# Attention in units twice as large, with masks as products, in a streaming-encoder step

## The chip, the cores and the metric

The kernel runs on one core of a Trainium2 chip. The metric is the device time of one execution in microseconds (us), from the first instruction to the last, with what the launch puts around it. PE is TensorE (matrix products), DVE is VectorE, ACT is ScalarE, POOL is GpSimd and SP is SyncE, which here only issues DMAs. PSUM, where PE writes, has eight banks of 128 partitions by 512 fp32 numbers.

## The reference, cut to what matters

One inference step over 256 prompt frames and 8 streams of 16 frames (384 rows in three blocks of 128; the third holds the streams) goes through a Mamba-2 layer and a PEER layer (a mixture of 16384 single-row experts), then an attention layer and a second PEER layer. Only attention changes:

```python
kv = rmsnorm(h, norm_kv) @ a_w_kv + a_b_kv        # 4 KV heads of 64
q = xn @ a_w_q[j] + a_b_q[j]                      # 16 query heads, 4 for each KV head
# prompt: chunks of 64 frames, a chunk sees itself and the two before it
scores = einsum('bcqkgd,bcskd->bckgqs', qb, kb) * scale
probs = sink_softmax(where(valid, scores, -inf), sinks)   # one more logit per head: the sink
out = einsum('bckgqs,bcskd->bcqkgd', probs, vb)
# streams: 16 queries against 128 cached rows and the 16 new ones
mix = o @ a_w_o[j] + a_b_o[j]
```

## The kernel before, in words

`mamba`, `peer(0)`, `attention`, `peer(1)` and `final` follow each other. A large fp32 product is made of three fp32r products, with each operand split into a high and a low part (`split`, L105 on ACT and L106 on DVE); their products are 128x128 weights against 256 to 512 moving columns and are called wide here. A framework orders the instructions of each engine in advance from its own estimate of their durations; those in `pin(...)` keep the order in which they are written, among themselves.

A PEER layer ends with 128 steps over the second expert table (`v_step`, products on L143) mixed with gathered rows for the streams (`v_quad`, L1089) and, in its first half, with sums that DVE makes of gathered rows (L1072) and of one-hot rows (`w_step`, L1111 to L1133). Near its end `h`, which was spilled to HBM, is read back (L1228).

Attention normalises `h`, transposes it and makes keys and values (`kv_block`, L143), then query tiles of 128 columns (`q_tile`, L130 to L132, 24 wide products each). POOL issues the loads of its constants first of all (L609 to L622): biases, sinks, the cached keys `ck` and values `cv`, and the output bias row `bo`. The body of attention goes over units. A prompt unit is two of the four query heads of a KV head, for one block of 128 rows, with 128 or 256 keys; there are 16. A unit of a stream is two KV heads with their eight query heads, 128 rows against 256 keys; there are 16. Each unit has `scores` (L719 on 64 of the 128 rows of the array; L728 and L729 on 64 rows and 64 columns), the mask addition on DVE out of PSUM into `sm` (L722, L731), `softmax` (maximum L693 on DVE, exponentials L700 on ACT, division L705 on DVE), `transposes` four units later (L741, copied out by ACT on L744) and `values` five units later (L758 and L771, weights of 64 columns). These products are called narrow here, and the transposes are counted with them. Six query tiles are written between the first scores. At the end the output projection runs (wide, L143 with `ohi`).

Of the kernel before, what the change touches and what calls it, by code (L numbers as in the profile page):

```python
# [9 lines left out]
F32 = mybir.dt.float32  # L10
# [9 lines left out]
P = 128  # L20
# [38 lines left out]
def encoder_step(ctx: ExitStack, tc: tile.TileContext, t_in, t_out):  # L59
# [543 lines left out]
    def attention():  # L603
        with ExitStack() as c:
# [4 lines left out]
            pool.dma_start(bq, t_in["b_q"])  # L609
            bkv = brow(t_in["b_kv"], 512, one, "bkv", pool)  # L610
            snk = brow(t_in["sinks"], 16, one, "snk", pool)
            nsnk = T(one, [P, 16], F32, tag="nsnk")
            dve.tensor_scalar(nsnk, snk, -1.0, None, op0=OP.mult)
            snks = T(one, [P, 2], F32, tag="snks")
            pool.dma_start(snks, t_in["sinks_s"])
            nsnks = T(one, [P, 2], F32, tag="nsnks")
            dve.tensor_scalar(nsnks, snks, -1.0, None, op0=OP.mult)
            ck = T(one, [64, NSEQ, 4, P], F32, tag="ck")
            cv = T(one, [P, NSEQ, 256], F32, tag="cv")
            pool.dma_start(ck, t_in["ckT"])  # L620
            pool.dma_start(cv, t_in["cache_v"].rearrange("s k d -> k s d"))
            bo = brow(t_in["b_o"], D, one, "bo", pool)  # L622

            mask0 = T(one, [P, P], F32, tag="mask0")
            pool.memset(mask0, 0.0)
            pool.memset(mask0[0:64, 64:128], NEG)
            mask1 = T(one, [P, NP], F32, tag="mask1")
            pool.memset(mask1, 0.0)
            pool.memset(mask1[0:64, 192:256], NEG)
            pool.memset(mask1[64:128, 0:64], NEG)  # L630
            maskS = T(one, [P, NSEQ, NP], F32, tag="maskS")
# [14 lines left out]
            r = rstd_of(h, DONE)  # L646
            accs = [[bank([P, 512])] for _ in range(NB)]
# [42 lines left out]
            def softmax(sm, sink, nsink, nh, nk):  # L690

                nm = T(two, [P, 2], F32, tag="nm", bufs=6)[:, :nh]
                dve.tensor_reduce(nm, sm, axis=AX.X, op=OP.max)  # L693
                dve.scalar_tensor_tensor(nm, nm, -0.125, nsink, op0=OP.mult, op1=OP.min)
                es = T(two, [P, 2], F32, tag="es", bufs=6)[:, :nh]
                dve.tensor_tensor(es, sink, nm, op=OP.add)
                act.activation(es, es, AF.Exp)
                den = T(two, [P, 2], F32, tag="den", bufs=6)[:, :nh]
                for i in range(nh):
                    act.activation(sm[:, i], sm[:, i], AF.Exp, bias=nm[:, i:i + 1], scale=0.125,  # L700
                                   accum_out=den[:, i:i + 1])
                dve.tensor_tensor(den, den, es, op=OP.add)
                dve.reciprocal(den, den)
                for i in range(nh):
                    dve.tensor_scalar(sm[:, i], sm[:, i], den[:, i:i + 1], None, op0=OP.mult)  # L705


            P_, PT = {}, {}
            LAG = 4

            def scores(u):
                kind, i, n, par = u
                sm = T(two, [P, 512], F32, tag="sm", bufs=LAG + 2)
                if kind == "p":
                    nk = (P, NP)[i]
                    hf = slice(64 * par, 64 * par + 64)
                    ps = bank([P, 2, nk])
                    for j in range(2):
                        pe.matmul(ps[:, j], qT[hf, 2 * n + j, i * P:(i + 1) * P], kT[hf, n, 0:nk],  # L719
                                  start=True, stop=True)  # L720
                    sm = sm[:, :2 * nk].rearrange("p (n k) -> p n k", k=nk)
                    dve.tensor_tensor(sm, ps, (mask0, mask1)[i].unsqueeze(1).to_broadcast([P, 2, nk]), op=OP.add)  # L722
                    softmax(sm, snk[:, 4 * n + par:4 * n + 4:2], nsnk[:, 4 * n + par:4 * n + 4:2], 2, nk)
                else:
                    ps = bank([P, NP])
                    for h2 in range(2):
# [620 lines left out]
```

## Time and profile before

| | |
|---|---|
| three runs | 2575.7, 2599.0, 2598.19 us; median 2598.19 us |
| the profiled execution | 2597.6 us, its span 2595.9 us |
| TensorE's granted clock, mean | 0.976 of 2.4 GHz |
| PE busy | 2449.1 us, 94% |
| DVE busy | 1941.7 us, 75% |
| ACT busy | 1323.8 us, 51% |
| POOL busy | 685.0 us, 26% |
| body of attention, first scores to output projection | 1440.57 to 1547.80 us |

In the table of stretches a row gives the stretch, its length, the busy time of each engine with the number of instructions in brackets, TensorE's granted clock as a share of 2.4 GHz, the share of time in which the DMA engines were busy, and what they moved. The clock has two levels, so 0.79 is a mean over time at 1.00 and at 0.50. In the rows by time, the second number is the duration with its drain; the time to the start of the next row is what a group costs PE when nothing waits.

### The profile page before, as it was taken

How to read it: one execution, taken by the hardware profiler on the slowest of the kernel's cores; microseconds unless marked ns; L12 is line 12 of the kernel's file. 1: busy time of each engine (PE TensorE's matmuls, PEld its weight loads, DVE VectorE, ACT ScalarE, POOL GpSimd, SP SyncE). 2: the span in 40 equal slices, each digit the busy share in tenths (PEclk: the TensorE clock that was granted, in tenths of full speed). 3: DMA queues.
4: the chain of work that ended last, by engine and by line, in shares of the span. 5: the costliest groups of instructions: out<-in, count | busy, mean ns of one | idle time of the engine just before them, and what ended most of it. 6: DMA issues, size and time to landing. Idle time of an engine off the chain costs nothing. (4 is left out here: it accounts for less than half of the span.)

```text
span 2595.9 us, 45141 instructions
## 1 busy us (share of the span) xinstructions
PE 2449.1 (94%) x16792; PEld 2070.4 (80%) x16792; DVE 1941.7 (75%) x4301; ACT 1323.8 (51%) x2562; POOL 685.0 (26%) x749
## 2 busy tenths in 40 slices
PE   7999999999899989999998999999899998899998
PEld 7999988988799966666666878998789976666666
DVE  6877737989899988765545655989989988775545
ACT  5655524433466665554444543434456666464444
POOL 2222200033322244333321100023332234433331
PEclk9999999999999999999998969999999999999999
DMA  4544444488888899888985204478888898988886
GB/s 182 203 148 178 144 135 145 151 282 273 271 305 293 292 340 349 330 308 296 322 307 179 92 9 150 137 253 280 269 286 287 296 323 311 364 294 294 321 315 233
DMA packets 179116, 645.62 MB, mean 249 GB/s; under 512 B 24192, under 2 KB 26096, under 8 KB 176240
## 3 DMA queue, kind: packets, MB, share of 16 engines
q1 hardware_dynamic: 99632, 366.90, 40.2%
q0 software_dynamic: 79264, 275.84, 30.5%
q8 instruction: 131, 2.15, 0.3%
q14 instruction: 89, 0.73, 0.1%
HBM read 626.43 MB, written 18.06 MB: 248 GB/s over the span
## 5 line engine op out<-in xcount | busy, mean ns | idle before, releaser
L105 ACT CAST hi<-raw 128x1024 fp32r<-128x1024 f32 (+1 forms) x616 | 641.3, 1042 | 652.8 <-PE bank L131 407.4
L106 DVE TENSOR_TENSOR lo<-raw,hi 128x1024 fp32r<-128x1024 f32 (+1 forms) x616 | 748.8, 1216 | 225.2 <-ACT hi L105 213.6
L1035 POOL DMA_INDIRECT gath<-in_p_u,eidU x256 | 301.9, 1179 | 803.3 <-DVE gath L1072 438.8
L132 PE MATMUL bank<-xhi,lo 128*128 128x256 f32 (+1 forms) x1344 | 407.5, 304 | 9.9 <-DVE lo L106 9.7
L130 PE MATMUL bank<-xhi,hi 128*128 128x256 f32 (+1 forms) x1344 | 402.3, 299 | 4.2 <-ACT hi L105 4.2
L131 PE MATMUL bank<-xlo,hi 128*128 128x256 f32 (+1 forms) x1344 | 396.7, 295 | 0.0
L132 PE MATMUL bank<-qhi,lo 128*128 128x256 f32 (+1 forms) x1152 | 348.9, 305 | 27.1 <-DVE lo L106 26.9
L130 PE MATMUL bank<-qhi,hi 128*128 128x256 f32 (+1 forms) x1152 | 348.1, 302 | 20.4 <-ACT hi L105 13.6
L1072 DVE SCALAR_TENSOR_TENSOR gath<-gath,xg 128x1024 f32<-128x1024 f32 x256 | 311.5, 1217 | 44.0 <-DMA gath<-in_p_u,eidU 43.9
L131 PE MATMUL bank<-qlo,hi 128*128 128x256 f32 (+1 forms) x1152 | 343.9, 299 | 0.0
L143 PE MATMUL bank<-lo,phi 128*128 128x512 f32 x1024 | 332.3, 406 | 10.2 <-DVE lo L106 8.2
L143 PE MATMUL bank<-hi,plo 128*128 128x512 f32 x1024 | 323.9, 398 | 0.0
L143 PE MATMUL bank<-hi,phi 128*128 128x512 f32 x1024 | 292.8, 406 | 19.4 <-ACT hi L105 16.1
L105 ACT CAST phi<-G 128x256 fp32r<-128x256 f32 x256 | 103.4, 405 | 382.0 <-PE bank L143 264.4
L1035 POOL DMA_INDIRECT gv<-in_p_v,eidT x180 | 202.1, 1123 | 319.0 <-PE bank L1089 273.6
L132 PEld LDWEIGHTS bank<-xhi,lo 128*128 128x128 f32 x1344 | 253.8, 189 | 18.0 <-DVE lo L106 14.1
L143 PEld LDWEIGHTS bank<-hi,phi 128*128 128x128 f32 x1024 | 186.9, 190 | 98.7 <-ACT hi L105 45.6
L130 PEld LDWEIGHTS bank<-xhi,hi 128*128 128x128 f32 x1344 | 254.3, 189 | 8.6 <-ACT hi L105 5.6
L131 PEld LDWEIGHTS bank<-xlo,hi 128*128 128x128 f32 x1344 | 254.1, 189 | 0.2
L132 PEld LDWEIGHTS bank<-qhi,lo 128*128 128x128 f32 x1152 | 222.9, 194 | 34.0 <-DVE lo L106 33.7
L143 PEld LDWEIGHTS bank<-lo,phi 128*128 128x128 f32 x1024 | 187.4, 190 | 73.2 <-DVE lo L106 18.3
L130 PEld LDWEIGHTS bank<-qhi,hi 128*128 128x128 f32 x1152 | 223.7, 194 | 24.3 <-ACT hi L105 16.7
(340 smaller groups left out, 3949.0 us busy)
## 6 DMA issues: line engine op xcount, KB each, us to landing
raw<-in_u_t SPq DMA_DIRECT2D x256, 512.0 KB
raw<-in_p_v SPq DMA_DIRECT2D x256, 512.0 KB
raw<-in_w_in SPq DMA_DIRECT2D x32, 512.0 KB
raw<-in_p_w_q SPq DMA_DIRECT2D x32, 512.0 KB
s<-in_state_ssm SPq DMA_DIRECT2D x8, 1024.0 KB
raw<-in_w_z SPq DMA_DIRECT2D x16, 512.0 KB
out_sm_ssm<-s SPq DMA_DIRECT2D x8, 1024.0 KB
raw<-in_w_out SPq DMA_DIRECT2D x16, 512.0 KB
```

The source lines that it names most:

```text
L105: act.copy(hi, raw)
L106: dve.tensor_tensor(lo, raw, hi32, op=OP.subtract)
L130: pe.matmul(ps, whi[:, s], xhi[:, k, c0:c1], start=(k == 0), stop=False)
L131: pe.matmul(ps, whi[:, s], xlo[:, k, c0:c1], start=False, stop=False)
L132: pe.matmul(ps, wlo[:, s], xhi[:, k, c0:c1], start=False, stop=(k == KD - 1))
L143: mm = pe.matmul(ps, x, w[:, hf * n:(hf + 1) * n], start=s_, stop=e_)
L1035: pool.indirect_dma_start(out=tile_, out_offset=None, in_=tab, in_offset=bass.IndirectOffsetOnAxis(ap=idx, axis=0))
L1072: pin(dve.scalar_tensor_tensor(tile_, tile_, 1.0, xg[g], op0=OP.mult, op1=OP.mult, accum_out=au[g][:, j:j + 1]))
```

## The change

A unit is twice as large: a prompt unit holds all four heads of a KV head, with a PSUM bank for the heads of each row half, and a unit of streams holds two streams in one bank; 16 units are left. Transposes come two units later and values three. The masks are bf16, and PE adds them: an identity (`idb`) times the mask starts the accumulation in the bank, and the scores go on top. DVE takes the maximum and ACT the exponentials straight from PSUM. Prompt scores alternate between the row halves of the array, values between its column halves, and the products of streams likewise. Of the two PSUM copies behind the transposes of a prompt unit DVE makes one. The products of units are pinned in the order masks, transposes, scores, values; query tiles stand behind units 0, 1, 3, 5, 7 and 8. The loads of constants are issued behind the normalisation's POOL work, and the masks are built before. The buffers of the output projection are reserved earlier.

```diff
-            bq = T(one, [P, 8], F32, tag="bq")
-            pool.dma_start(bq, t_in["b_q"])
...
+            def constants():
...
+                pin(pool.dma_start(bq, t_in["b_q"]))
+                row(bkv, t_in["b_kv"])
+                row(snk, t_in["sinks"])
+                pin(pool.dma_start(snks, t_in["sinks_s"]))
+                pin(pool.dma_start(ck, t_in["ckT"]))
+                pin(pool.dma_start(cv, t_in["cache_v"].rearrange("s k d -> k s d")))
+                row(bo, t_in["b_o"])
+            idb = T(one, [P, P], BF16, tag="idb")
+            dve.tensor_copy(idb, ident)
+            mask0 = T(one, [P, 2, P], BF16, tag="mask0")
...
             r = rstd_of(h, DONE)
+            constants()
+            dve.tensor_scalar(nsnk, snk, -1.0, None, op0=OP.mult)
+            dve.tensor_scalar(nsnks, snks, -1.0, None, op0=OP.mult)
...
+            LAG = 2
+            def masks(u):
+                kind, i, n = u
+                if kind == "p":
+                    m = (mask0, mask1)[i]
+                    SC[u] = [bank(m.shape) for _ in range(2)]
+                else:
+                    m = maskS[:, 2 * i:2 * i + 2]
+                    SC[u] = [bank([P, 2, NP])]
+                for ps in SC[u]:
+                    pin(pe.matmul(ps, idb, m, start=True, stop=False))
+            def scores(u):
+                kind, i, n = u
+                pss = SC.pop(u)
+                if kind == "p":
+                    nk = (P, NP)[i]
+                    for j in range(2):
+                        for par in range(2):
+                            hf = slice(64 * par, 64 * par + 64)
+                            pin(pe.matmul(pss[par][:, j], qT[hf, 2 * n + j, i * P:(i + 1) * P], kT[hf, n, 0:nk],
+                                          start=False, stop=(j == 1)))
...
+                for q, ps in enumerate(pss):
+                    dve.tensor_reduce(nm[:, q], ps, axis=AX.X, op=OP.max)
...
+                        act.activation(sm[:, j], ps[:, j], AF.Exp, bias=nm[:, q, j:j + 1], scale=0.125,
+                                       accum_out=den[:, q, j:j + 1])
...
+            def transposes(u):
+                for q, sm in enumerate(P_.pop(u)):
+                    pt = bank([P, 2, nkb, P])
...
+                    if q:
+                        dve.tensor_copy(pT, pt)
+                    else:
+                        act.copy(pT, pt)
...
+                    po = bank([P, 2, P])
                     for j in range(2):
+                        for kb in range(nkb):
+                            for h2 in range(2):
+                                pin(pe.matmul(po[64 * h2:64 * h2 + 64, j], kv[:, kb, 256 + n * 64:256 + (n + 1) * 64],
+                                              pT[h2][:, j, kb], start=(kb == 0), stop=(kb == nkb - 1)))
...
+            q_at = {0: 2, 1: 3, 3: 4, 5: 5, 7: 6, 8: 7}
...
+            for i in range(len(todo) + LAG + 1):
...
+                if i < len(todo):
+                    masks(todo[i])
+                if 0 <= i - LAG < len(todo):
+                    transposes(todo[i - LAG])
+                if i < len(todo):
+                    scores(todo[i])
+                if 0 <= i - LAG - 1 < len(todo):
+                    values(todo[i - LAG - 1])
+                if i in q_at:
+                    q_tile(q_at[i])
```

Three places show how the order moves, names with the numbers of their buffers. On PE, before, the last of the six query tiles (L130 to L132) ends early in the body, and narrow products alone follow it; the scores of nine and a half of the 16 prompt units and of all 16 units of streams are still to come, and the transposes and values of most:

```order
L131 MATMUL bank_15891<-xlo_2733_15298,hi_15894 128x384
L132 MATMUL bank_15891<-xhi_2732_15297,lo_15895 128x384
L719 MATMUL bank_15931<-kT_15261,qT_15257 128x256
L741 MATMUL bank_15948<-ident_69,sm_15712 128x128 x4
L758 MATMUL bank_15955<-pT_15871,kv_15258 64x128
L758 MATMUL bank_15955<-pT_15928,kv_15258 64x128
L758 MATMUL bank_15959<-pT_15871,kv_15258 64x128
L758 MATMUL bank_15959<-pT_15928,kv_15258 64x128
L719 MATMUL bank_15964<-kT_15261,qT_15257 128x256 x2
```

Every row from the third on is narrow, up to the output projection.

Now, on PE behind the last but one query tile (bank_16075, written behind unit 7); L717 is the mask, L770 a transpose, L727 a score:

```order
L132 MATMUL bank_16075<-xhi_2733_15299,lo_16079 128x384
L717 LDWEIGHTS idb_15230
L717 MATMUL bank_16109<-mask_2711_15232,idb_15230 128x256
L717 LDWEIGHTS idb_15230
L717 MATMUL bank_16110<-mask_2711_15232,idb_15230 128x256
L770 MATMUL bank_16113<-ident_69,sm_16007 128x128 x4
L727 MATMUL bank_16109<-kT_15254,qT_15250 128x128
L727 MATMUL bank_16110<-kT_15254,qT_15250 128x128
```

The query tiles now lie among the first nine units; the last one follows this unit, and seven units of scores come behind it. The masks come ahead of the transposes, and the scores go to two banks in turn.

On POOL at the border of the first PEER layer and attention, before:

```order
L1035 DMA gv_14923<-in_p_v,eidT_4013 128x1024
L609 DMA bq_15221<-in_b_q 128x8
L81 DMA bkv_15223<-in_b_kv 128x512
L81 DMA snk_15225<-in_sinks 128x16
L615 DMA snks_15229<-in_sinks_s 128x2
L620 DMA ck_15233<-in_ckT 64x4096
L621 DMA cv_15234<-in_cache_v 128x8x256
L81 DMA bo_15237<-in_b_o 128x1024
L625 MEMSET mask_2710_15239 128x128
```

and now:

```order
L645 MEMSET maskS_15239 128x16 x8
L168 TENSOR_TENSOR rstd_15263<-ss_15261,mhalf_78 128x1 x3
L623 DMA bq_15221<-in_b_q 128x8
L621 DMA bkv_15222<-in_b_kv 128x512
L621 DMA snk_15223<-in_sinks 128x16
L626 DMA snks_15225<-in_sinks_s 128x2
L627 DMA ck_15227<-in_ckT 64x4096
L628 DMA cv_15228<-in_cache_v 128x8x256
L621 DMA bo_15229<-in_b_o 128x1024
L696 DMA out_pr_k<-kv_15251 128x256
```

The loads moved behind all three reciprocal roots (`rstd`), which close the first PEER layer.

The framework also reorders the second PEER layer's last stage, which the edit does not touch. On DVE, in its first half, before:

```order
L106 TENSOR_TENSOR plo_24410<-G_3096_17048,phi_24409 128x256
L1072 SCALAR_TENSOR_TENSOR gath_24293,au_21565<-gath_24293,xg_3113_17093 128x1024
L1111 TENSOR_TENSOR ob_24727<-ioh_76,e1T_17040 128x512
L106 TENSOR_TENSOR lo_24406<-raw_24403,hi_24405 128x1024
L106 TENSOR_TENSOR plo_24453<-G_3096_17048,phi_24452 128x256
```

and now:

```order
L106 TENSOR_TENSOR plo_24204<-G_3001_16842,phi_24203 128x256
L1109 SCALAR_TENSOR_TENSOR gath_24087,au_21359<-gath_24087,xg_3018_16887 128x1024
L1148 TENSOR_TENSOR ob_24521<-ioh_76,e1T_16834 128x512
L106 TENSOR_TENSOR plo_24247<-G_3001_16842,phi_24246 128x256
L1109 SCALAR_TENSOR_TENSOR gath_24164,au_21359<-gath_24164,xg_3018_16887 128x1024
L1170 SCALAR_TENSOR_TENSOR G_3615_20399<-bank_24440,G_3615_20399 128x64x8
L1164 TENSOR_TENSOR oa_24539<-ioh_76,e2T_16835 128x512
L1151 TENSOR_TENSOR og_24523<-ob_24521,g_2998_16836 128x1024
L106 TENSOR_TENSOR lo_24200<-raw_24197,hi_24199 128x1024
```

One low part (`lo`) of an expert row moved behind five other DVE instructions; the rows after it are interleaved in another way too.

## Rows read from the trace of the kernel before

**Rows 1.** Table of stretches: the body of attention and four parts of it.

```profile
1440.57:1547.80 107.23, 104.89 (x769) 80.54 (x768) 68.91 (x266) 58.33 (x210) 0.00 (x0) 0.79 0.11 35
1440.57:1476.50 35.93, 35.93 (x197) 31.49 (x196) 22.90 (x69) 18.43 (x50) 0.00 (x0) 1.00 0.27 88
1476.50:1492.70 16.20, 13.92 (x156) 10.11 (x154) 13.65 (x62) 11.59 (x47) 0.00 (x0) 1.00 0.10 34
1492.70:1537.50 44.80, 44.74 (x244) 30.89 (x244) 27.00 (x111) 21.93 (x88) 0.00 (x0) 0.50 0.00 1
1537.50:1547.80 10.30, 10.30 (x176) 8.04 (x174) 5.35 (x26) 6.39 (x27) 0.00 (x0) 1.00 0.01 3
```

**Rows 2.** Table of stretches: the last 100 products of each PEER layer.

```profile
1369.00:1401.00 32.00, 26.42 (x100) 19.25 (x97) 13.92 (x24) 10.89 (x20) 8.04 (x24) 0.89 0.76 236
2562.60:2587.20 24.60, 23.48 (x100) 17.64 (x96) 14.57 (x23) 11.30 (x20) 1.15 (x2) 1.00 0.56 199
```

**Rows 3.** Waits, 1369 to 1401 us: waiter, what ended it, us, times, longest.

```profile
ACT hi L105 <- DMA raw<-in_p_v: 7.8, 2, 6.2
```

**Rows 4.** Waits, 2562.6 to 2588 us, the second layer's counterpart.

```profile
ACT hi L105 <- DMA raw<-in_p_v: 0.9, 1, 0.9
```

**Rows 5.** PE by time: start, duration, engine, line, names; prompt scores and what follows.

```profile
1445.64 0.71 PE L719 MATMUL bank<-kT,qT 64*128 64x128 f32 x4
1446.28 0.44 PE L130 MATMUL bank<-xhi,hi 128*128 128x384 f32 x1
...
1450.70 1.13 PE L719 MATMUL bank<-kT,qT 64*128 64x256 f32 x4
1451.76 0.45 PE L130 MATMUL bank<-xhi,hi 128*128 128x384 f32 x1
```

**Rows 6.** PE by time: stream scores, transposes and values at the full clock.

```profile
1478.53 0.44 PE L728 MATMUL bank<-ck,qs 64*64 64x128 f32 x4
...
1479.12 0.44 PE L741 MATMUL bank<-ident,sm 128*128 128x128 f32 x2
1479.49 1.09 PE L758 MATMUL bank<-pT,kv 128*64 128x128 f32 x8
1480.51 0.44 PE L728 MATMUL bank<-ck,qs 64*64 64x128 f32 x4
...
1482.40 0.66 PE L758 MATMUL bank<-pT,kv 128*64 128x128 f32 x8
1482.99 0.44 PE L728 MATMUL bank<-ck,qs 64*64 64x128 f32 x4
...
1483.58 0.66 PE L741 MATMUL bank<-ident,sm 128*128 128x128 f32 x4
1484.16 0.44 PE L728 MATMUL bank<-ck,qs 64*64 64x128 f32 x4
```

**Rows 7.** PE by time: wide products of 512 columns, full clock.

```profile
2579.66 0.63 PE L143 MATMUL bank<-lo,phi 128*128 128x512 f32 x2
2580.13 0.63 PE L143 MATMUL bank<-hi,plo 128*128 128x512 f32 x2
```

**Rows 8.** Groups of instructions on DVE, body of attention: busy us, mean ns; idle before.

```profile
L722 DVE TENSOR_TENSOR sm<-bank,mask 128x256 f32<-128x256 f32 (+1 forms) x16 | 8.9, 556 | 11.3 <-PE bank L719 11.3
L731 DVE TENSOR_TENSOR sm<-bank,maskS 128x256 f32<-128x256 f32 x16 | 6.7, 423 | 14.5 <-PE bank L729 14.5
```

**Rows 9.** Groups by form, the same stretch: an exponential and a maximum.

```profile
L700 ACT ACTIVATE sm<-sm,nm 128x256 f32<-128x256 f32 x32 | 16.1, 505 | 4.6 <-DVE nm L694 4.5
L693 DVE TENSOR_REDUCE nm<-sm 128x2 f32<-128x512 f32 x8 | 5.5, 684 | 0.1
```

**Rows 10.** DMA issues, 1360 to 1400 us: one of the constants.

```profile
ck<-in_ckT POOLq DMA_DIRECT2D x1, 1024.0 KB
```

**Rows 11.** Table of stretches: keys and values up to the query tiles.

```profile
1401.00:1430.00 29.00, 24.43 (x107) 19.42 (x105) 20.02 (x35) 16.07 (x30) 1.20 (x3) 0.88 0.32 102
```

**Rows 12.** Table of stretches: the second PEER layer's last stage, first half.

```profile
2104.00:2350.00 246.00, 223.69 (x1470) 151.19 (x1468) 187.92 (x317) 139.90 (x276) 103.58 (x94) 0.99 0.90 327
```

**Rows 13.** Groups by form on DVE, that first half: low parts of expert rows.

```profile
L106 DVE TENSOR_TENSOR lo<-raw,hi 128x1024 fp32r<-128x1024 f32 x59 | 72.2, 1225 | 8.2 <-ACT hi L105 5.7 <-issue 2.4
```

More of the change, by code (lines that the diff above doesn't have):

```diff
@@ L694, in softmax @@
                 dve.scalar_tensor_tensor(nm, nm, -0.125, nsink, op0=OP.mult, op1=OP.min)
-                es = T(two, [P, 2], F32, tag="es", bufs=6)[:, :nh]
                 dve.tensor_tensor(es, sink, nm, op=OP.add)
                 act.activation(es, es, AF.Exp)
[L698 to L701, printed above, removed]
+                sms = []
@@ L703, in softmax @@
                 dve.reciprocal(den, den)
[L704 to L713, printed above, removed]
-                if kind == "p":
[L715 to L726, printed above, removed]
-                        lhs = qs[:, i, 2 * n + h2].rearrange("p g t -> p (g t)")
-                        pe.matmul(ps[64 * h2:64 * h2 + 64, 0:P], lhs, ck[:, i, 2 * n + h2], start=True, stop=True)
-                        pe.matmul(ps[64 * h2:64 * h2 + 64, P:], lhs, kT[0:64, 2 * n + h2, NP:], start=True, stop=True)
-                    sm = sm[:, :NP].rearrange("p (n k) -> p n k", n=1)
-                    dve.tensor_tensor(sm[:, 0], ps, maskS[:, i], op=OP.add)
-                    softmax(sm, snks[:, n:n + 1], nsnks[:, n:n + 1], 1, NP)
-                P_[u] = sm
@@ L735, in transposes @@
-            def transposes(u):
-                sm = P_.pop(u)
-                nh, nkb = sm.shape[1], sm.shape[2] // P
-                pt = bank([P, nh, nkb, P])
-                for j in range(nh):
-                    for kb in range(nkb):
-                        pe.transpose(pt[:, j, kb], sm[:, j, kb * P:(kb + 1) * P], ident)
-                pT = T(two, [P, 512], F32, tag="pT", bufs=4)[:, :nh * nkb * P].rearrange(
-                    "p (n k q) -> p n k q", k=nkb, q=P)
-                act.copy(pT, pt)
-                PT[u] = pT
@@ L753, in values @@
+            def values(u):
+                kind, i, n = u
+                pT = PT.pop(u)
+                if kind == "p":
+                    po = bank([P, 2, P])
                     nkb = (1, 2)[i]
                     for j in range(2):
-                        po = bank([P, P])
-                        for h2 in range(2):
-                            for kb in range(nkb):
-                                pe.matmul(po[64 * h2:64 * h2 + 64, :], kv[:, kb, 256 + n * 64:256 + (n + 1) * 64],
-                                          pT[h2][:, j, kb], start=(kb == 0), stop=(kb == nkb - 1))
@@ L795, in attention, with out_terms @@
-            with tc.tile_pool(name="a3", bufs=1) as late:
-                ohi = T(late, [P, 8, NT], F32R, tag="ohi")
-                olo = T(late, [P, 8, NT], F32R, tag="olo")
+                    todo += [("s", s, n // 2) for s in range(NSEQ // 2)]
+            q_at = {0: 2, 1: 3, 3: 4, 5: 5, 7: 6, 8: 7}
+            late = c.enter_context(tc.tile_pool(name="a3", bufs=1))
+            ohi = T(late, [P, 8, NT], F32R, tag="ohi")
+            olo = T(late, [P, 8, NT], F32R, tag="olo")
+            def out_terms():
@@ L810, in peer @@
+            accs = [[bank([P, 512]) for _ in range(2)] for _ in range(NB)]
+            gemm_row_loop(accs, out_terms())
+            for b in range(NB):
+                for hf in range(2):
+                    hh = h[:, b, hf * 512:(hf + 1) * 512]
+                    dve.tensor_tensor(hh, hh, accs[b][hf], op=OP.add)
     def peer(l):
```

121 lines of the change are left out of this document (61 added, 60 removed).

## The prediction

> **What bounds the kernel now.** The page first: TensorE is busy 94% of the span, so a change elsewhere counts only where PE waits or runs slowly. Then the table of stretches over the part that is edited. The body of attention takes 107.23 us, of which PE is busy 104.89; DVE is busy 68.91 and ACT 58.33 of it, so PE bounds it [rows 1]. The reader should then look at the clock column: 1.00 up to 1492.7 us, 0.50 for 44.8 us, 1.00 after that. PE did 44.74 us of work in the slow part, which is 22.37 us at the full clock. The body is thus 82.5 us of PE work at the full clock (104.89 - 22.37), 2.3 us of idle PE (107.23 - 104.89), and 22.4 us of clock. What PE did before the clock fell is in the same rows: 35.9 us without a gap, query tiles and narrow products mixed, and then 16.2 us of narrow products alone, in which it worked 13.92 us. The second place is the end of the first PEER layer: its last 100 products take 32.0 us, the same 100 in the second layer 24.6 us [rows 2]. The waits say why: ACT waits 7.8 us for rows of the expert table in the first and 0.9 us in the second [rows 3, 4]. The constants of attention load in just that stretch, 1 MB for the cached keys alone [rows 10].
>
> **The sum, against the profiled execution's 2597.6 us** (the median of the runs is 2598.2, so the two agree).
>
> *Constants later.* The seven loads leave the last experts of the first PEER layer. The gain there is the difference of the waits, 6.9 us (7.8 - 0.9); the lengths of the two stretches differ by 7.4. The loads now start behind the third root and run beside keys and values. Their sizes add up to 2.8 MB (1 MB each for keys and values, 0.5 for the output bias, 0.25 for the key-value bias, the rest small); at the 236 GB/s of the border they need 12 us. In the 29 us after it the DMA engines were busy 0.32 of the time [rows 11], which leaves 19.7 us free. So they fit, though some key-value weights will share the engines with them. I charge 1 us and take **-6**; the ends are 0 (all of it given back) and -7.4. The two negations of sinks on DVE now wait for a small load that POOL issues late; behind them stand the low parts of the normalised rows. They are among the first instructions of a stage in which PE has some 5 us of slack (24.43 of 29 busy [rows 11]), and the 1 us covers that.
>
> *Prompt scores.* Two matmuls on one row half cost PE 0.64 us with 128 keys (1446.28 - 1445.64) and 1.06 with 256 [rows 5], and there are two such units for each new one. In the new order the halves alternate. No row shows row halves in turn; the nearest is the value products, where eight records on one column half at a time cost 1.02 us and eight in turn 0.59 [rows 6], a ratio of 0.58. At that ratio a new unit costs 0.74 for 1.28 (saves 0.54) and 1.23 for 2.12 (saves 0.89). Four units of each kind: -5.7. Ends: 0, if row halves don't overlap, and -6.8 at a clean half.
>
> *Values.* Prompt units of 128 keys alternate already in part, so nothing. Those of 256 keys have two such groups of eight, 2 x 1.02, and go to 2 x 0.59: -0.86 each, four units, -3.4. Value products of streams stay as many as before, on halves of 64 columns; nothing. Ends for values: 0 and -4.
>
> *Transposes and scores of streams.* Each group of narrow products ends with a drain. Two transposes cost 0.37 us and four cost 0.58 [rows 6], so joining two groups of two saves 0.16, joining two of four about as much. Twelve units (four with 128 keys, eight of streams) save 0.16, four save 0.14, and the eight joined stream scores (0.59 a group) some 0.15: -3.7 in all.
>
> *Masks on PE.* A wide product of 512 columns costs 0.235 us (2580.13 - 2579.66 for two) [rows 7]. The four units of 256 keys have two masks of that width, the eight of streams one, the four of 128 keys two of half the width: (4 x 2 + 8 + 4) x 0.235 = **+4.7**. A bf16 mask could be cheaper or, with its own weights to load, dearer: 0 to +8.
>
> *What leaves DVE.* The mask additions, 8.9 and 6.7 us [rows 8], and half of the short instructions on columns. DVE's sum stays below PE's, so this is priced at nothing; its cover is PE, and if PE waited for DVE it would be worth at most its 15.6 us. One copy of four prompt units in each kind goes from ACT to DVE, again under PE.
>
> *Idle PE.* The narrow work is then 82.5 - 5.7 - 3.4 - 3.7 + 4.7 = 74.4 us, query tiles included. Units are larger and the lag is two units instead of four, and a prompt unit now takes five of the eight banks, two for scores, two for transposes, one for values. So a transpose or a value product may get a bank that the last unit's exponentials still read. I take 6 us of idle instead of 2.3, the ends being 2.3 and the price of a rival below.
>
> *Clock.* In the new order the six query tiles lie among the first nine units instead of ahead of nearly everything, and every unit has masks as wide as the array. The likeliest is that the clock holds: 22.4 us of clock go to 0. The body takes 74.4 + 6 = 80.4 us, against 107.2: **-26.8**.
>
> *The second PEER layer.* The order of its last stage changes although the edit does not touch it. The work is the same, the interleaving another; I count 0, with 5 us to either side, a quarter of the 22.3 us for which PE idles there now (246.0 - 223.69) [rows 12].
>
> Sum: 2597.6 - 6 - 26.8 = **2564.8 us**, say 2565. With its own ends it lies between 2556 and 2574.
>
> **Rivals.**
>
> *The clock falls again.* For it: in the rows above it fell with PE busy 86% of the stretch, and came back only after 44.8 us in which PE was busy throughout. Seven units of scores and the work of two more still follow the last query tile. By the same prices that is some 25 us of PE work. If the clock holds for 16.2 us, as before, and then halves for the rest, about 11 to 13 us are added: **2577**. Against it: masks of full width in between and halves used together. The runs of before (2575.7 beside 2599) differ by 23 us, about what the clock cost in the profiled one, which would fit if it held in one run of three; no trace shows that run.
>
> *The softmax becomes the bound.* PSUM is read by DVE for the maximum, 0.68 us for 512 columns, and by ACT for the exponentials, 0.5 us each [rows 9]. If each new unit's banks hold PE until they have been read, a prompt unit of 256 keys costs it 2 x 0.68 + 4 x 0.5 = 3.4 us, one of 128 about 2.6, one of streams 1.7: 38 us together, of which query tiles and the values of other units cover perhaps a quarter. With 29 us of idle instead of 6 the sum is **2588**. The Trainium skill, TensorEngine Tiling (Array Packing), section Performance Considerations, says that tiling speeds up TensorE but not the emptying of PSUM, which may become the bottleneck. By that rule this rival is the case. The trace of before speaks for PE by sums (DVE 68.91 of 107.23 us [rows 1]), but not by latencies.
>
> *The last stage of the second PEER layer loses more than attention gains*: slower than before. The low part of an expert row (1.2 us of DVE [rows 13]) now stands, at one place, behind five instructions that it stood ahead of. If that went on for the whole stage, PE would wait for one such instruction at each of the 59 experts of the first half, 72 us, and the time would be **2637**. It decides at 0.55 us each, 33 us, where all that I forecast is eaten up. Against it: the same DVE work fits (187.92 of 246.0 us [rows 12]), and an instruction that is late once does not make the following ones late.
>
> *Better than forecast:* clean halves, no new idle and all 7.4 us of the constants, with the clock up: **2555**.
>
> **How the numbers follow.** Chances: forecast 0.48, clock 0.30, softmax 0.11, second PEER layer 0.06, better 0.05. The time is that of the likeliest, 2565, with its own range 2556 to 2574. The range for 8 in 10 takes in the clock's case with its spread and the better case to 2553, and leaves out the slower case and half of the softmax's: 2553 to 2588. About 1% is what a measurement of this kernel can tell from no change, 26 us here, so faster means below 2572. That holds for nearly nine tenths of the forecast (0.43), a fifth of the clock's case (0.07) and the better one (0.05): 0.55. Slower, above 2624, is most of the second PEER layer's case: 0.05. The rest, 0.40, is within 1%.
>
> **What the profile of the changed kernel would show.** The last 100 products of the first PEER layer should take about 25 us with no wait of ACT for expert rows above 1 us; if keys and values get longer by as much, the constants were only moved. In the body PE should be busy 74 to 75 us at clock 1.00; eight prompt score records in turn should cost no more than four do now; masks should be 24 products, 16 near 0.23 us and 8 near half of it. If the clock column shows 0.50 behind the last query tile, the first rival holds; if PE waits there for exponentials or maxima, the second. If the second PEER layer's last stage is longer than now, the third. The forecast is wrong by its main term if the clock falls in the body for more than 10 us.

## The result and the profile after

The changed kernel takes 2571.26 us (median of 8 runs, 2561.69 to 2583.0), the kernel before 2594.72 us (8 runs, 2575.7 to 2601.01). The ratio is 0.9919, with a 95% interval of 0.9891 to 0.9947: faster by 0.5 to 1.1%, across the mark of 1% that the prediction set. The forecast was 2565 us, with a range of 2553 to 2588. The kernel before had been put at 2597.6, so the forecast gain was 33 us; by the medians 23.5 came.

The profiled execution of the changed kernel takes 2576.9 us, 20.7 less than the one before. By stages, between the same products of both traces:

| stage | before, us | after, us | difference |
|---|---|---|---|
| start to the last stage of the first PEER layer (not edited) | 919.6 | 926.8 | +7.2 |
| last stage of the first PEER layer | 481.3 | 472.0 | -9.3 |
| to the body of attention | 39.7 | 42.4 | +2.7 |
| body of attention | 107.2 | 84.3 | -22.9 |
| output projection and second PEER layer | 1048.1 | 1049.6 | +1.5 |

The first row is scatter between executions: over the 14 profiles of this study it lies between 919.0 and 927.5 us, with the same instructions, and TensorE stands at half clock for 20.5 to 37.5 us of it (before 23.9, after 34.1). The second row holds scatter too: in the 12 profiles with the large constants late it takes 471.5 to 480.6 us, in the two with all of them early 481.3 and 484.6.

The table of stretches after, for the body and four parts of it; [rows 1] stand against it. The columns are as there.

```profile
1441.20:1525.56 84.36, 77.02 (x794) 64.27 (x793) 53.66 (x170) 47.37 (x169) 0.00 (x0) 0.92 0.14 45
1441.20:1489.90 48.70, 46.54 (x411) 40.58 (x410) 32.77 (x101) 27.43 (x93) 0.00 (x0) 1.00 0.21 66
1489.90:1505.70 15.80, 12.22 (x158) 8.80 (x156) 11.98 (x37) 11.18 (x42) 0.00 (x0) 1.00 0.12 35
1505.70:1519.40 13.70, 12.49 (x84) 9.81 (x86) 6.95 (x25) 5.80 (x22) 0.00 (x0) 0.50 0.01 1
1519.40:1525.56 6.16, 5.76 (x147) 5.09 (x143) 1.96 (x7) 2.96 (x13) 0.00 (x0) 1.00 0.01 3
```

Taken apart as the prediction did it: PE is busy 77.02 us, of which 12.49 at half clock count 6.25 at the full one, so the work is 70.8 us; idle is 84.36 - 77.02 = 7.3; the clock costs 6.2. Before, these were 82.5, 2.3 and 22.4 us: 11.7 us of the gain are work and 16.2 clock, and 5.0 us of idle time are lost. The clock still falls behind the last query tile (which ends at 1489.9), after 15.8 us in which PE worked 12.22, but for 13.7 us instead of 44.8.

PE's waits in the body (waiter, what ended the wait, us, times, longest), and the row of PE with the longest one:

```profile
PE bank L770 <- DVE sm L760: 5.2, 3, 3.8
PE bank L727 <- ACT qT L677: 2.2, 1, 2.2
```

```profile
1506.91 1.94 PE L770 MATMUL bank<-ident,sm 128*128 128x128 f32 x8 [3.81 <-DVE sm L760]
```

No wait is for a bank. The long one is for the softmax of the last prompt unit, and DVE by time shows what stood in it:

```profile
1499.75 1.02 DVE L106 TENSOR_TENSOR olo<-oT,ohi 128x384 fp32r<-128x384 f32 x2
1500.68 0.69 DVE L744 TENSOR_REDUCE nm<-bank 128x2 f32<-128x512 f32 x1
1501.29 0.55 DVE L106 TENSOR_TENSOR olo<-oT,ohi 128x384 fp32r<-128x384 f32 x1
1501.75 0.69 DVE L744 TENSOR_REDUCE nm<-bank 128x2 f32<-128x512 f32 x1
1502.35 0.55 DVE L106 TENSOR_TENSOR olo<-oT,ohi 128x384 fp32r<-128x384 f32 x1
1502.82 0.42 DVE L774 COPY pT<-bank 128x256 f32<-128x256 f32 x1
1503.15 0.68 DVE L744 TENSOR_REDUCE nm<-bank 128x2 f32<-128x512 f32 x1
1503.75 0.16 DVE L745 SCALAR_TENSOR_TENSOR nm<-nm,nsnk 128x4 f32<-128x4 f32 x1
```

The scores were done at 1499.4, as the rows of PE show:

```profile
1498.26 1.13 PE L727 MATMUL bank<-kT,qT 64*128 64x256 f32 x8
1499.32 0.66 PE L788 MATMUL bank<-pT,kv 128*64 128x128 f32 x8
```

`nm` is a unit's maximum; L744 appears for that unit and the one after it, and L745 closes the first. Four low parts (`olo`) of the output projection's operands, 2.1 us, stand between the scores and the exponentials, and beside them a copy and the next unit's maximum, 1.1 us together. The low parts are wanted only from 1525.6 on. The change reserves their buffers early, and the framework put them there.

The end of the first PEER layer answers to [rows 2]: 24.6 us instead of 32.0, and the 7.8 us of ACT's waits for expert rows [rows 3] are gone.

```profile
1374.70:1399.30 24.60, 23.75 (x101) 17.79 (x97) 15.01 (x24) 11.20 (x20) 4.80 (x17) 1.00 0.59 195
```

What is given back stands in the waits of keys and values, which have no counterpart before:

```profile
DVE nsnk L658 <- DMA snk<-in_sinks: 3.5, 1, 3.5
ACT hi L105 <- DMA raw<-in_w_kv: 3.0, 2, 1.8
DVE nsnks L659 <- DMA snks<-in_sinks_s: 1.3, 1, 1.3
PEld bank L143 <- DVE xlo L109: 1.4, 1, 1.4
PE bank L143 <- DVE xlo L109: 1.0, 1, 1.0
```

The last two are PE and its weight loads (PEld) waiting for the low parts of the normalised rows (`xlo`), which stand behind the two negations on DVE.

### The profile page after: what moved, and what is told of

Same layout as the page of the kernel before. It is cut to its first block, busy times and chain, and to the rows that moved or that the text cites. A ratio compares the mean times of both kernels' runs of the same rounds, so it can differ in the third digit from the quotient of the medians.

```text
span 2575.2 us, 45047 instructions
## 1 busy us (share of the span) xinstructions
PE 2425.7 (94%) x16816; PEld 2055.6 (80%) x16816; DVE 1927.6 (75%) x4206; ACT 1313.5 (51%) x2522; POOL 683.2 (27%) x749
## 5 line engine op out<-in xcount | busy, mean ns | idle before, releaser
L132 PE MATMUL bank<-xhi,lo 128*128 128x256 f32 (+1 forms) x1344 | 408.3, 304 | 12.6 <-DVE lo L106 12.5
L130 PE MATMUL bank<-xhi,hi 128*128 128x256 f32 (+1 forms) x1344 | 404.2, 301 | 4.2 <-ACT hi L105 4.2
L132 PE MATMUL bank<-qhi,lo 128*128 128x256 f32 (+1 forms) x1152 | 349.0, 305 | 29.7 <-DVE lo L106 29.5
L130 PE MATMUL bank<-qhi,hi 128*128 128x256 f32 (+1 forms) x1152 | 348.3, 303 | 19.6 <-ACT hi L105 12.0
L143 PE MATMUL bank<-hi,phi 128*128 128x512 f32 x1024 | 291.6, 405 | 16.8 <-ACT hi L105 13.6
L132 PEld LDWEIGHTS bank<-xhi,lo 128*128 128x128 f32 x1344 | 255.4, 190 | 20.0 <-DVE lo L106 17.6
L130 PEld LDWEIGHTS bank<-xhi,hi 128*128 128x128 f32 x1344 | 255.9, 190 | 8.8 <-ACT hi L105 5.2
L132 PEld LDWEIGHTS bank<-qhi,lo 128*128 128x128 f32 x1152 | 223.3, 195 | 36.5 <-DVE lo L106 36.2
L130 PEld LDWEIGHTS bank<-qhi,hi 128*128 128x128 f32 x1152 | 223.7, 194 | 23.5 <-ACT hi L105 15.1
```

Source lines behind the costliest of these rows:

```text
L130: pe.matmul(ps, whi[:, s], xhi[:, k, c0:c1], start=(k == 0), stop=False)
L132: pe.matmul(ps, wlo[:, s], xhi[:, k, c0:c1], start=False, stop=(k == KD - 1))
L143: mm = pe.matmul(ps, x, w[:, hf * n:(hf + 1) * n], start=s_, stop=e_)
```

## Experiments

Body, work at the full clock, idle PE, the time at half clock inside the body and the stretch ahead of it (from the last product of the first PEER layer) are taken from each profile as above, in us; ratios are to the kernel before on the same chip. There is one profile of each kernel; the ratios are from 4 to 12 runs.

| kernel | body | work | idle | at half clock | to the body | ratio (95%) |
|---|---|---|---|---|---|---|
| change | 84.3 | 70.8 | 7.3 | 13.7 | 42.4 | 0.9919 (0.9891 to 0.9947) |
| split_late | 77.4 | 71.4 | 6.0 | 0 | 42.3 | 0.9880 (0.9854 to 0.9906) |
| q_early | 83.9 | 70.9 | 7.1 | 13.6 | 43.0 | 0.9905 (0.9871 to 0.9939) |
| const_early | 86.0 | 70.3 | 8.0 | 17.1 | 39.6 | 0.9950 (0.9932 to 0.9968) |
| before_const_late | 102.6 | 83.3 | 2.3 | 34.1 | 42.8 | 0.9972 (0.9952 to 0.9992) |
| masks_dve | 89.4 | 65.5 | 9.7 | 30.2 | 42.5 | 0.9915 (0.9885 to 0.9946) |
| no_turns | 79.6 | 72.5 | 5.5 | 3.4 | 42.1 | 0.9867 (0.9839 to 0.9894) |
| small_early | 77.5 | 71.6 | 5.9 | 0 | 38.5 | 0.9860 (0.9838 to 0.9882) |
| mixed_units | 80.3 | 71.2 | 1.8 | 14.7 | 38.7 | 0.9844 (0.9821 to 0.9867) |
| lag3 | 77.6 | 71.8 | 4.1 | 3.4 | 42.2 | 0.9875 (0.9851 to 0.9898) |
| tile3 | 83.0 | 70.9 | 8.3 | 10.0 | 38.7 | 0.9902 (0.9881 to 0.9923) |
| wide_fill | 79.4 | 78.9 | 0.5 | 0 | 38.6 | 0.9896 (0.9873 to 0.9920) |
| best | 74.5 | 71.9 | 1.4 | 2.4 | 38.5 | 0.9875 (0.9843 to 0.9907) |

**The wait ahead of the fall: split_late.**

```diff
+                if i == len(todo) - 1:
+                    for ct in range(4):
+                        pin(act.copy(ohi[:, ct], oT[:, ct]))
+                        pin(dve.tensor_tensor(olo[:, ct], oT[:, ct], ohi[:, ct].bitcast(F32), op=OP.subtract))
                 if 0 <= i - LAG - 1 < len(todo):
                     values(todo[i - LAG - 1])
...
-                    split(ohi[:, ct], olo[:, ct], oT[:, ct])
+                    if ct > 3:
+                        split(ohi[:, ct], olo[:, ct], oT[:, ct])
```

> The changed kernel, with the output projection's operand splits of the first four tiles put behind the last softmax. In the changed kernel four of them (2.1 us of DVE) stand between the maxima of the last prompt unit, PE then waits 3.8 us for that softmax, and the clock falls for 13.7 us right behind. Theory A (the wait causes the fall): the wait shrinks to about 1.7 us, the clock stays at 1.00 in the body, the body goes from 84.4 to about 76 us and the time falls by about 8 us. Rival B (the clock falls because only narrow products follow the last query tile): the wait shrinks, the clock falls all the same for about 14 us; body about 82 us, time lower by 2 us.

In this profile theory A held: the clock is at 1.00 throughout, and the body is 77.4 us. The interval of the ratio overlaps that of the change, so the time alone does not show the gain. The longest wait for a softmax is 1.1 us.

```profile
1444.70:1522.20 77.50, 71.50 (x793) 59.89 (x793) 53.35 (x171) 47.23 (x169) 0.00 (x0) 1.00 0.16 49
1493.40:1522.20 28.80, 25.13 (x385) 19.32 (x383) 20.59 (x69) 19.77 (x76) 0.00 (x0) 1.00 0.07 20
```

The second row begins where the last query tile ends: 28.8 us of masks and narrow products, busy 87%, and no fall.

**Where the query tiles stand: q_early.**

```diff
-            q_at = {0: 2, 1: 3, 3: 4, 5: 5, 7: 6, 8: 7}
+            q_at = {0: 2, 1: 3, 2: 4, 3: 5, 4: 6, 5: 7}
```

> The changed kernel with the six query tiles behind units 0 to 5 instead of 0, 1, 3, 5, 7, 8. Theory A (idle PE ahead of the fall): the last ten units lose two covers of 4.2 us each, PE waits for softmax 3 to 6 us more, and the clock falls where the waits are; body 90 to 95 us. Rival B (narrow products alone): two more tiles' worth of units is narrow, the clock falls some 16 us behind the last query tile and stays low for 30 us or more; body 97 us or more. Rival C (spreading the query tiles does nothing): body 84 us as before.

Rival C held: the body is as in the change. The clock fell 25 us behind the last query tile, for 13.6 us, next to a wait of 3.6 us like the one in the change. So narrow products alone did not make it fall 16 us behind the tile, and the spreading that I counted on brought nothing that can be seen.

```profile
1478.00:1503.00 25.00, 20.54 (x294) 15.46 (x292) 20.48 (x66) 17.28 (x68) 0.00 (x0) 1.00 0.07 23
1503.00:1516.60 13.60, 11.66 (x79) 9.32 (x82) 6.32 (x23) 6.08 (x25) 0.00 (x0) 0.50 0.00 1
```

**The constants: const_early, before_const_late.** In the first, `constants()` stands ahead of the masks in the changed kernel, and the negations of sinks stay where they are. In the second, the kernel before gets it behind the roots, with the negations.

```diff
+            constants()
             idb = T(one, [P, P], BF16, tag="idb")
...
             r = rstd_of(h, DONE)
-            constants()
```

> The changed kernel with the loads of constants at their old place, ahead of the masks and the roots. If the late loads give what the traces show: the last 100 products of the first PEER layer go back from about 25 to 32 us with some 7 us of ACT waiting for expert rows, keys and values get 2 to 2.5 us shorter, and the time rises by 5 us. Rival (the difference was scatter between executions): both stretches stay, and the time with them.

> The kernel before with nothing changed but the loads of constants, issued behind the third root as in the change. If constants are worth what the prediction says: last 100 products of the first PEER layer 25 us instead of 32, keys and values 1 to 2.5 us longer, body of attention unchanged (107 us with the clock low for some 40 us), time lower by 5 to 6 us. Rival (given back in keys and values): both terms cancel, time unchanged.

With early loads ACT waits again for expert rows at the end of the first PEER layer:

```profile
ACT hi L105 <- DMA raw<-in_p_v: 7.0, 2, 4.9
```

There the last stage of that layer takes 484.6 us against 472.0 in the change, and the stretch to the body 39.6 against 42.4. The kernel before with late loads has no such wait; its stage takes 478.5 us against 481.3, its stretch to the body 42.8 against 39.7. Those two terms cancel (-2.8 and +3.1); its ratio of 0.9972 is 7 us, but its body was shorter, with 34 us at half clock instead of 44. In the changed kernel the two terms make 12.6 - 2.8 = 9.8 us, and the two ratios (0.9950 and 0.9919) lie 8 us apart. The wait is taken away as expected; the net gain is between 0 and 10 us, and the scatter of the stage is as large.

**What gives it back: small_early.** Only `ck`, `cv` and `bo` are loaded late, on top of split_late.

```diff
+            pool.dma_start(bq, t_in["b_q"])
+            row(bkv, t_in["b_kv"])
+            row(snk, t_in["sinks"])
+            pool.dma_start(snks, t_in["sinks_s"])
+            dve.tensor_scalar(nsnk, snk, -1.0, None, op0=OP.mult)
+            dve.tensor_scalar(nsnks, snks, -1.0, None, op0=OP.mult)
             def constants():
-                pin(pool.dma_start(bq, t_in["b_q"]))
...
                 pin(pool.dma_start(ck, t_in["ckT"]))
```

> The kernel split_late with the four small constants (two biases, two of sinks, 0.27 MB) loaded at the old place and only the cached keys and values and the output bias behind the roots. In split_late DVE waits 3.4 and 1.3 us for the sinks ahead of the low parts of normalised rows, and keys and values take 42.3 us against 39.7 before. If those waits make the difference: keys and values 40 us, time lower by 2 to 3 us than split_late. If the loads' share of the DMA engines makes it (ACT waits 3.6 us for key-value weights): 42 us as now, no gain. The end of the first PEER layer stays at 26.5 us for the last 100 products, or grows by 1 us for the 0.27 MB.

The stretch to the body falls from 42.3 to 38.5 us, below the 39.7 of the kernel before, and the last stage of the first PEER layer takes 473.0 us, 472.0 in the change. ACT still waits 2.4 us there for key-value weights (3.6 in split_late), so most of what was given back was probably DVE's wait for two loads of 8 KB and 1 KB; the two biases were moved with them, and no run moves the sinks alone. The runs do not separate it from split_late.

**Turns between the halves: no_turns.** In split_late, loops are exchanged, here for prompt scores.

```diff
-                    for j in range(2):
-                        for par in range(2):
+                    for par in range(2):
+                        for j in range(2):
```

> The kernel split_late with the narrow products of a unit one half after the other again: scores of one row half, then of the other; values of one column half, then of the other. If it is the turns that save: prompt scores go from 0.64 and 1.06 us back to 1.28 and 2.12 (6.8 us over eight units), values of 256 keys from 1.02 to about 2.0 (3.6 us), streams little; PE's work in the body rises by about 10 us, body 77.4 to 86 or 88. If the larger units alone save: work unchanged, body 77 us.

The rival held: the work rises by 1.1 us, not by 10. The rows of PE, no_turns first, then split_late:

```profile
1448.85 0.72 PE L727 MATMUL bank<-kT,qT 64*128 64x128 f32 x8
1449.50 0.44 PE L131 MATMUL bank<-xlo,hi 128*128 128x384 f32 x1
...
1472.66 1.15 PE L788 MATMUL bank<-pT,kv 128*64 128x128 f32 x16
1473.73 0.39 PE L717 MATMUL bank<-maskS,idb 128*128 128x512 bf16 x1
```

```profile
1446.80 0.71 PE L727 MATMUL bank<-kT,qT 64*128 64x128 f32 x8
1447.44 0.44 PE L131 MATMUL bank<-xlo,hi 128*128 128x384 f32 x1
...
1468.81 1.09 PE L788 MATMUL bank<-pT,kv 128*64 128x128 f32 x16
1469.83 0.39 PE L717 MATMUL bank<-maskS,idb 128*128 128x512 bf16 x1
```

Eight records of 128 keys cost 0.64 or 0.65 us in either order, as much as four did before [rows 5]. The two row halves work at once when the products of both stand in one unit; their turn within it hardly matters.

**Masks: masks_dve.** In split_late, DVE adds the masks out of PSUM; the scores start their banks.

```diff
-                for ps in SC[u]:
-                    pin(pe.matmul(ps, idb, m, start=True, stop=False))
...
+                    dve.tensor_tensor(sm, ps, msk, op=OP.add)
+                    dve.tensor_reduce(nm[:, q], sm, axis=AX.X, op=OP.max)
```

> The kernel split_late with the masks added by DVE again (out of PSUM into sm, maximum and exponentials from there) and no mask products. PE is spared 4.4 us (16 products at 0.22 us, 8 at 0.11), DVE gets about 15 us more, 0.7 to 1.5 us of it in each unit's chain. Theory M (the wide mask products between the narrow ones are what keeps the clock up): the clock falls behind the last query tile for 15 us or more, body 82 us or more against 77.4. Theory A (only waits of PE make it fall): body 73 to 78 us with the clock at 1.00 as long as no wait is longer than about 2 us; if the longer chain makes waits of 3 us or more, it falls right behind one of them.

PE is spared 5.9 us, and still the body is 12 us longer: PE waits 4.9 and 3.0 us for the longer softmax, and the clock falls around both and stays low for the last 19.9 us (3.4 us more come early). Theories A and M both foresaw this, so the run does not part them. It shows what taking the masks off PE costs in this order, not by which way.

```profile
PE bank L770 <- DVE sm L760: 7.9, 2, 4.9
```

**Less idle time: mixed_units, and wide work added to it: wide_fill.** In mixed_units, which is small_early in another order, stream units stand between the later prompt units and tile 3 behind tile 2; wide_fill adds useless products.

```diff
-                if n % 2:
-                    todo += [("s", s, n // 2) for s in range(NSEQ // 2)]
+            for at, u in ((4, ("s", 0, 0)), (5, ("s", 1, 0)), (7, ("s", 2, 0)), (9, ("s", 3, 0)), (11, ("s", 0, 1))):
+                todo.insert(at, u)
+            todo += [("s", s, 1) for s in range(1, NSEQ // 2)]
-            q_at = {0: 2, 1: 3, 3: 4, 5: 5, 7: 6, 8: 7}
+            q_at = {0: (2, 3), 2: (4,), 4: (5,), 6: (6,), 8: (7,)}
```

```diff
+                wide = bank([P, 512])
+                if todo.index(u) >= 8:
+                    for _ in range(4):
+                        pin(pe.matmul(wide, idb, maskS[:, 0:2], start=True, stop=True))
...
```

> The kernel small_early with the units in another order: the four stream units of the first heads one at a time between the later prompt units, one of the second heads between the last two prompt units, and query tile 3 directly behind tile 2 (PE waits 2.2 us for it in split_late). If the idle 6 us of the body come from prompt softmaxes in a row and from tile 3: idle falls to 2 to 3 us, body 77.4 to 74, clock at 1.00, time lower by 3 us than small_early. Rival: the waits move to the tail, which has fewer stream units to cover it; body the same.

> The kernel mixed_units with four useless mask products of 512 columns (results overwritten) ahead of the values of each of the last eight units: 32 x 0.22 = 7 us more PE work at the full clock. In mixed_units the clock fell 18 us behind the last query tile with PE never idle for more than 1.3 us and stayed low to the end of the body (14.7 us, 7.4 us lost). Theory N (a stretch with too little wide work lets it fall): the clock stays at 1.00 and the body is 80 us as before, the added work paid for by the clock. Theory T (it falls some 15 to 20 us behind the last query tile whatever PE does): the clock is low again for 14 us or more, body 87 us or more.

The idle time fell to 1.8 us as expected, and the clock fell all the same, with no wait above 1.3 us ahead of it. Theory A, as the only cause, falls with that. In wide_fill the clock stays up for 32 us behind the last query tile: theory N held, theory T did not. But the added products also covered PE's last waits (0.2 us in the body, 1.8 in mixed_units), so the run does not part their width from the missing waits. PE's waits of mixed_units, its stretches from the last query tile to the fall and from there to the end of the body, then the stretch from the last query tile in wide_fill:

```profile
PE bank L770 <- DVE sm L760: 1.8, 3, 1.3
```

```profile
1485.40:1503.80 18.40, 16.61 (x219) 12.46 (x217) 13.34 (x47) 12.67 (x48) 0.00 (x0) 1.00 0.10 30
1503.80:1518.50 14.70, 14.70 (x178) 12.56 (x174) 6.08 (x20) 6.58 (x24) 0.00 (x0) 0.50 0.01 2
```

```profile
1491.40:1523.50 32.10, 31.64 (x419) 22.15 (x422) 19.18 (x66) 19.34 (x72) 0.00 (x0) 1.00 0.06 18
```

The body of wide_fill is as long as that of mixed_units (79.4 and 80.3 us): 7.7 us of added work against 7.4 us of clock. As a kernel it gains nothing.

**A longer lag: lag3.** `LAG = 3` in the changed kernel, the splits where they were.

> The changed kernel with transposes three units after the scores instead of two; the operand splits stay where they are. One more unit (about 2.6 us of PE) covers each softmax. If the wait of 3.8 us is the softmax's latency: it falls to about 1.2 us, body 84.4 to about 80 us if the clock still falls, about 75 if it does not. mixed_units has shown a fall with no wait above 1.3 us ahead of it, so a fall is open here: if the wait is what matters in this order of units, the clock stays at 1.00. Rival: five of eight banks for one unit make PE wait for banks instead, body 84 us or more.

The longest wait for a softmax is 1.4 us and the tail stays at 1.00 (3.4 us at half clock come early, beside the wait for tile 3). Body 77.6 us, where 75 were expected with the clock up; it is the same as split_late by another way. The row is from the last query tile to the end of the body.

```profile
1491.70:1519.00 27.30, 25.75 (x418) 20.82 (x418) 19.65 (x69) 20.57 (x79) 0.00 (x0) 1.00 0.07 22
```

**Tile 3: tile3.** In small_early, `q_at = {0: (2, 3), 3: (4,), 5: (5,), 7: (6,), 8: (7,)}`.

> The kernel small_early with query tile 3 directly behind tile 2, ahead of the second unit; the order of units as in the change. PE's wait of 2.2 us for that tile goes, the tail is the same, so the clock should stay at 1.00: body 77.5 to about 75.3 us, time 2 us below small_early. Rival: the first unit's transposes come 4.2 us of cover earlier and wait for their softmax instead, body 77 us.

The rival's wait came: that of 2.2 us went and one of 4.5 us appeared, since the cover left the place where the transposes of an early unit needed it. Body 83.0 us, where the rival had 77: the clock fell for 6.8 us at that wait, and again at the end of the tail. That tail is the one of small_early, with no wait above 1.2 us in either, and there the clock held.

```profile
1459.68 1.94 PE L770 MATMUL bank<-ident,sm 128*128 128x128 f32 x8 [4.50 <-DVE sm L760]
```

From the last query tile to this fall, and from there to the end of the body:

```profile
1495.00:1521.90 26.90, 23.23 (x326) 17.53 (x326) 19.86 (x68) 18.93 (x74) 0.00 (x0) 1.00 0.07 21
1521.90:1525.10 3.20, 3.20 (x64) 3.17 (x62) 0.76 (x2) 0.81 (x3) 0.00 (x0) 0.51 0.02 5
```

**All of it: best.** tile3 with `LAG = 3`.

> The version that the runs point to: the changed kernel with the operand splits behind the last softmax, the small constants at the old place, query tile 3 behind tile 2, and transposes three units after the scores. In tile3 the first unit's transposes waited 4.5 us for their softmax; with one more unit of lag that wait should be covered by the 4.2 us of a query tile, or by scores. Expected: idle of PE in the body 2 to 3 us, body 73 to 75 us if the clock stays at 1.00, 80 if it falls in the tail as in mixed_units; keys and values 38.6 us; time 2 to 4 us below small_early, a ratio of about 0.985 to the kernel before.

```profile
1435.40:1509.80 74.40, 73.04 (x793) 61.29 (x792) 52.16 (x170) 46.83 (x169) 0.00 (x0) 0.98 0.16 51
```

The shortest body of all, 74.5 us with 1.4 us idle; the clock falls for its last 2.4 us and costs the output projection 2 us more (36.3 instead of 34.3). The median is 2562.15 us, the ratio 0.9875 (0.9843 to 0.9907), where 0.985 was expected. It is faster than the kernel before; that it beats split_late, lag3, small_early or mixed_units is not shown, their intervals overlap. Of all these kernels only small_early and mixed_units have an interval wholly below that of the change.

## Why the prediction came out as it did

The time fell into the range and on the forecast side, 6 us above the forecast. That is partly luck: the main term, the clock, failed by the mark set for it, while the work came out smaller than forecast, and the kernel before measured 3 us less than the sum began from. The steps, against the profiled execution:

- **Constants, -6 forecast.** Traces of before and after give -9.3 and +2.7, -6.6. The wait was removed as forecast; that the sum is so near is partly luck, as the stage scatters by 9 us with late loads. The step that failed is "the 1 us covers that" for the negations of sinks: DVE waited 4.8 us for their loads, the low parts behind them came late, and small_early, with the biases early too, is 3.8 us shorter there than split_late. PE's slack in the stage was no cover, because PE waits for those low parts.
- **Prompt scores, -5.7 by turns.** The unit of 128 keys costs 0.64 us and that of 256 costs 1.06, the end of a clean half: -6.8. The size was near, the reason was not: no_turns shows that joining the units does it, and the turns hardly matter.
- **Values, transposes, masks.** The work forecast was 74.4 us, it is 70.8, counting the scores. A mask of 512 columns takes 0.22 us (two in 0.44) where 0.235 was put in; two groups of eight value records take 1.02 us together where 1.18 was put in (1.09 with its drain in split_late's row, 1.02 to the next). Values of streams, put at nothing, went from 2 x 0.61 us to 1.06 for two streams, 1.3 us over eight units. With the 1.1 us of the scores these make 3.3 of the 3.6 us. The rows, of the change (two masks of 512, values of two streams) and then of before (values of one):

```profile
1456.17 0.60 PE L717 MATMUL bank<-mask,idb 128*128 128x512 bf16 x2
1456.61 1.04 PE L770 MATMUL bank<-ident,sm 128*128 128x128 f32 x8
...
1492.07 0.31 PE L801 MATMUL bank<-pT,cv 128*64 128x32 f32 x4
...
1493.13 0.39 PE L717 MATMUL bank<-mask,idb 128*128 128x256 bf16 x2
```

```profile
1488.44 0.32 PE L771 MATMUL bank<-pT,cv 128*64 128x32 f32 x4
...
1489.05 0.44 PE L728 MATMUL bank<-ck,qs 64*64 64x128 f32 x4
```

- **Idle, 6 forecast, 7.3 measured.** The size is near by luck, for the cause is another. I put it down to banks still being read; no bank was waited for. It is the latency of the softmax with a lag of two units, with 2.1 us of operand splits in its way on DVE, and 2.2 us for query tile 3.
- **Clock, 0 forecast, 6.2 measured.** By its own mark (more than 10 us at half clock) the main term failed: the first rival, a fall behind the last query tile, took place at half its price of 11 to 13 us. The reason I gave for holding it, query tiles spread, is not borne out by q_early.
- **Softmax as the bound.** The rule cited from the Trainium skill, TensorEngine Tiling (Array Packing), Performance Considerations, is that emptying PSUM may become the limit; the page names this for a speedup of four, and what the rows show here is two halves at once. In this trace it is not the limit: with 29 us of idle it would have been so, PE idled 7.3, and DVE was busy 53.7 of 84.4 us. As a bound it did not come; as latency it made the wait ahead of the fall.
- **Second PEER layer, 0 +- 5.** Its last stage took 478.6 us against 477.6; over the 14 profiles it lies between 472 and 484, with no trend. The third rival did not occur.

The forecast of 2564.8 stands against 2576.9 for the profiled execution. To within rounding the 12.1 us are the scatter ahead of the edit (7.2), the clock (6.2), idle time (1.3) and the later stages (1.5), less the work (3.6) and the constants (0.6).

**What stays open.** What PE must have been doing for the clock to fall is not settled. Shown: the four profiles with a wait of 3.0 us or more behind the last query tile (the change, q_early, const_early, masks_dve) fell there for 13.6 us or more. Where that wait was taken away, the tail kept its clock in four profiles (split_late, no_turns, small_early, lag3) and fell late, for its last 2.4 to 3.2 us and on into the output projection, in two (tile3, best). In another order of units it fell without a long wait, and added wide products held it there. With one profile of each kernel, and with 20.5 to 37.5 us at half clock in the same instructions ahead of the edit, a fall of a few us may be chance. The kernel before fell after 16.2 us, busy 86% [rows 1], without masks on PE, at a wait of 1.5 us; split_late held for 28.8 us, busy 87%, with them. So busy time alone does not tell the two apart. That masks as products are what the change gained the clock by is possible and not shown, since masks_dve also lengthened the waits; so the reason for the largest part of the gain, 16.2 us, stays open. The row of before:

```profile
1492.76 0.49 PE L741 MATMUL bank<-ident,sm 128*128 128x128 f32 x2 [1.48 <-DVE sm L705]
```

## What to carry to other kernels

A stretch that runs at a lower clock is a term of its own: find what PE did ahead of it, both its waits and how wide its products were. Here, taking away the long wait was the surest step, and another order of the units lost the clock although no long wait was left. When buffers are reserved earlier, look in the order for work that is ready but not needed, standing inside a chain of latencies that another engine waits for. When large loads are put off, leave those of a few KB on which an engine's queue waits where they were.

## What the runs showed of the hardware

- Products on the two row halves of the array run at once when they follow each other in one group, whether in turn (0.64 us for eight records of 64x128 in split_late) or one half after the other (0.65 in no_turns): four records on one half alone cost 0.64 before [rows 5].
- PE at half clock came back to 1.00 while it still did narrow work, after 13.6 to 13.7 us with masks among it (the change, q_early), and after 44.8 us without [rows 1]; in mixed_units it stayed low through 14.7 us in which PE was never idle.
